# Backward scan: when the context tile's gate rows are loaded, where the output norm scales o, and which half is turned first

## The chip, the cores and the metric

The kernel runs on one core of a Trainium2 chip. It uses the core's engines: TensorE (PE) for matrix products and transposes (its weight loads are shown apart as PEld), VectorE (DVE), ScalarE (ACT) and GpSimd (POOL) for elementwise work, and SyncE (SP), which issues all DMAs. The metric is device microseconds of the whole program, measured over several runs; the profile is one more execution, taken by the hardware profiler.

## The reference

One layer of a hybrid backbone over 17 tiles of 128 tokens: tile 0 is context, tiles 1 to 16 are latent tokens. For each group of tokens:

```python
def block(x, s0, mod, n_chunks, ...):
    sh1, sc1, ga1, sh2, sc2, ga2 = mod
    h = rmsnorm(x, norm_mix_l) * (1.0 + sc1) + sh1
    o, s_new = mixer(h, s0, n_chunks, ...)
    x = x + ga1 * o
    h = rmsnorm(x, norm_ffn_l) * (1.0 + sc2) + sh2
    x = x + ga2 * (jnp.square(jax.nn.relu(h @ w_ff1_l)) @ w_ff2_l)
    return x, s_new
```

and the end of the mixer, which is the part that the change is about:

```python
    o_a, s_new = delta_bidir(q, k, v, g2, beta2, s0)      # DeltaNet, forward and backward
    o_a = rmsnorm(o_a, o_norm_l) * jax.nn.silu(gate.reshape(B, T, H_A, DV))
    ...
    o_b = u * mixed.reshape(B, T, D_B).astype(u.dtype)    # gated MLP over chunks
    out = jnp.concatenate([o_a.reshape(B, T, D_A).astype(h.dtype), o_b.astype(h.dtype)], axis=-1)
    return out @ w_out_l, s_new
```

Context tokens are modulated with another vector than latent tokens, so their gate row `ga1` is another one. `x` is 128 x 1024 a tile; `o_a` and `o_b` are 128 x 512 each, four heads (or groups) of 128.

## The kernel before

The program has three stages. The first projects all tokens and stores what the scans need in DRAM. The second is the scan: a forward pass over the tiles, then a backward pass. The third is the MLP, some 1,300 us of dense products. Products in single precision are made of three matmuls each (L220 to L222: high by high, low by high, high by low), so every operand is split into a rounded high part (on ACT) and the rest (on DVE).

The scan works in units, one for a tile and a direction: unit 0 and unit 1 are the context tile's two directions, units 2 to 17 go forward over the tiles 1 to 16, units 18 to 33 backward over 16 to 1. Each unit has a chain of four steps (`u["scan"]`) that carries the state, and a preparation made for two units together (`pair`): the triangular inverse, by doubling. For each width w of 2, 4, 8, 16 and 32 a level has two steps. The first multiplies on PE (L1173), and DVE copies the result under a mask into P (`copy_predicated`, L1176). The second multiplies with P on PE (L1187, L1193), and ACT copies the results to Y and X. Before the levels there are two turns of X (L1149). The first step for w = 16 is called P16 in what follows, by its copy.

Beside chain and preparation runs "fill": in the forward pass the projections of the gated MLP, in the backward pass the output of each finished tile. For a backward unit of tile t, `o_steps` makes that output:

- `norm` (from L1381) loads ob (the gated MLP's half, from DRAM), squares o on ACT and computes the norm's factors rr, the power by -0.5 on POOL (L178).
- `scaled` (L1396) makes the four factors complete (L1398, a 128 x 4 instruction) and multiplies o by factor and gate, in four instructions, one a head (L1400).
- `trans(0)` turns o, `trans(1)` turns ob: four transposes on PE into a PSUM bank (L1413), the high part on ACT (L1417), the low part on DVE (L1418). `trans(0)` also issues the loads of x (L1409).
- `proj(n, k0)`, eight steps: two halves n of 512 columns, four steps each, over the eight pieces k of the turned halves (0 to 3 are o's, 4 to 7 ob's). The last step of a half multiplies by the gate row into `tmp` (L1437), adds to x (L1438) and stores (L1440).

The gate row of latent tiles is loaded once (`ga1`). For the context tile (`cond(t) == 0`) the last step of each half loads a row of its own with `wrow` (L213): one row of 512 values to all 128 partitions, 256 KB in the tile.

PSUM banks come from `pj()`, which alternates between two pools of two banks, named pm and pj in the profile. Tiles of 512 columns in SBUF come from one pool of 49 (`wp`, tag "w"), which also holds the projection weights.

The order is written as due times. Each step is an event with a time in units: unit i's chain lies near i. A unit's output steps lie at i + 1.0 + part * 0.38, with the parts that `o_steps` returns, and its eight `proj` steps at i + 1.69 to i + 2.69. In that measure P16 of the pair of units i and i + 1 is due at 0.0625 after an odd unit's time, its second step at 0.1875; after an even unit's time the two turns of X lie there. The context tile's output steps are due at 17.9 + part * 0.4 and its `proj` steps from 17 + 1.5 to 17 + 2.68. `emit` issues the events in order of their times. A step without a matmul that is not "fill" is put behind the first matmul of the latest chain or preparation step before it (`hist[-1]`), on whichever engine it runs; a fill step's first matmul is put behind that one too. Within these bounds a planner with a simulated timeline fixes the order of each engine's instructions, earlier-issued ones first among those that are ready; on the chip each engine's queue then runs in that order. SP issues DMAs in its own such order, and a DMA that waits (for a buffer or for an earlier store) holds up those behind it.

Of the kernel before, what the change touches and what calls it, by code (L numbers as in the profile page):

```python
# [14 lines left out]
ALU = mybir.AluOpType  # L15
# [4 lines left out]
D = 1024  # L20
KT = D // P
# [3 lines left out]
H = 4  # L25
# [37 lines left out]
def hybrid_step(  # L63
# [7 lines left out]
    V, A, G, T = nc.vector, nc.scalar, nc.gpsimd, nc.tensor  # L71
# [3 lines left out]
    def xrow(t):  # L75
        return x_prompt[0] if t == 0 else x_sample[0, (t - 1) * P : t * P, :]
# [4 lines left out]
    def cond(t):  # L81
        return 0 if t == 0 else 1

    def f32(ap):
        return ap.bitcast(F32)
# [6 lines left out]
    mod_d = dp.tile([2, 6 * D], F32, name="mod_d")  # L92
# [56 lines left out]
    rq = cp.tile([P, NT, H], F32, name="rq")  # L149
# [24 lines left out]
    def rsqrt_cols(out, ss, n, scale, eps):  # L174
        t = smp.tile([P, 72], F32, tag="rsq", name="rsq", bufs=2)
        np_ = ss.shape[0]
        V.tensor_scalar(out=t[:np_, :n], in0=ss, scalar1=scale, scalar2=eps, op0=ALU.mult, op1=ALU.add)  # L177
        G.tensor_tensor(out=out, in0=t[:np_, :n], in1=nhalf[:np_, :n], op=ALU.pow)  # L178
# [28 lines left out]
    def w512(name, dt=F32):  # L207
        return wp.tile([P, 512], dt, tag="w", name=name)

    def wrow(row):  # L210

        t = w512("row")
        load(out=t, in_=row.to_broadcast([P, 512]))  # L213
        return t

    def mm3(ps, trip, first=True, last=True, more=False):

        n = len(trip)
        for i, (lh, ll, rh, rl) in enumerate(trip):
            T.matmul(ps, lh, rh, start=first and i == 0, stop=False, skip_group_check=more)  # L220
            T.matmul(ps, lh, rl, start=False, stop=False, skip_group_check=more)  # L221
            T.matmul(ps, ll, rh, start=False, stop=last and i == n - 1, skip_group_check=more)  # L222
# [58 lines left out]
    with ExitStack() as ph:  # L281
# [5 lines left out]
        def pj(dt=F32):  # L287
            return ppj.tile([P, 512], dt, tag="pj", name="pj", bufs=3)
# [471 lines left out]
        for bi in range(len(BLOCKS)):  # L760
# [8 lines left out]
            for n, (gi, h) in enumerate(order):  # L769
                u = us[n] if bi == 0 and n < 3 else feature_tile(blk, bi, gi, h)  # L770
# [156 lines left out]
    with ExitStack() as ph:  # L927
# [421 lines left out]
        ga1 = []  # L1349
# [26 lines left out]
        def o_steps(du):  # L1376
            t = du["t"]
            out = []
            u = {}

            def norm():  # L1381
                du["ob"] = w512("ob")
                load(out=du["ob"], in_=ob_d[t * P : (t + 1) * P, :])
                o, ga = du["o"], du["ga"]
                ss = smp.tile([P, 4], F32, tag="oss", name="oss")
                junk = fp.tile([P, P], BF16, tag="junk", name="junk", bufs=1)
                for h in range(H):
                    A.activation(junk, o[:, h, :], AF.Square, accum_out=ss[:, h : h + 1])
                r2 = smp.tile([P, 4], F32, tag="r2", name="r2")
                rr = smp.tile([P, 4], F32, tag="rr", name="rr")  # L1390
                V.tensor_tensor(out=r2, in0=rq[:, t, :], in1=rq[:, t, :], op=ALU.mult)
                V.tensor_tensor(out=r2, in0=r2, in1=ss, op=ALU.mult)
                rsqrt_cols(rr, r2, 4, 1.0 / P, EPS)
                u["rr"] = rr

            def scaled():  # L1396
                o, ga, rr = du["o"], du["ga"], u["rr"]
                V.scalar_tensor_tensor(out=rr, in0=rr, scalar=0.5, in1=rq[:, t, :], op0=ALU.mult, op1=ALU.mult)  # L1398
                for h in range(H):
                    V.scalar_tensor_tensor(out=o[:, h, :], in0=o[:, h, :], scalar=rr[:, h : h + 1],  # L1400
                                           in1=ga[:, h * P : (h + 1) * P], op0=ALU.mult, op1=ALU.mult)

            def trans(half):
                def f():
                    if half == 0:
                        u["H"], u["L"] = [], []
                        u["x"] = [w512("x"), w512("x")]
                        for n in range(2):
                            load(out=u["x"][n], in_=xrow(t)[:, n * 512 : (n + 1) * 512])  # L1409
                    src = du["o"] if half == 0 else du["ob"].rearrange("p (h d) -> p h d", h=H)  # L1410
                    ps = pj().rearrange("p (h d) -> p h d", h=H)
                    for h in reversed(range(H)):
                        T.transpose(ps[:, h, :], src[:, h, :], ident)  # L1413
                    hs = hp.tile([P, 4, P], F32R, tag="h", name="oH")
                    ls = hp.tile([P, 4, P], F32R, tag="h", name="oL")
                    scale = 0.5 if half else vec[:, 68:69]
                    A.activation(hs, ps, AF.Copy, scale=scale)  # L1417
                    V.scalar_tensor_tensor(out=ls, in0=ps, scalar=scale, in1=f32(hs), op0=ALU.mult, op1=ALU.subtract)  # L1418
                    u["H"] += [hs[:, i, :] for i in range(4)]
                    u["L"] += [ls[:, i, :] for i in range(4)]  # L1420
                return f

            def proj(n, k0):
                def f():
                    if k0 == 0:
                        u["ps"] = pj()
                    for k in (k0, k0 + 1):
                        mm3(u["ps"], [(u["H"][k], u["L"][k]) + WO[n][k]], first=k == 0,
                            last=k == KT - 1)
                    if k0 == KT - 2:  # L1430
                        sl = slice(n * 512, (n + 1) * 512)
                        tmp = fp.tile([P, 512], F32, tag="ug" if n else "vg", name="tmp")
                        ga = ga1[n]
                        if cond(t) == 0:
                            ga = wrow(mod_d[0:1, 2 * D + n * 512 : 2 * D + n * 512 + 512])
                        x = u["x"][n]
                        V.tensor_tensor(out=tmp, in0=u["ps"], in1=ga, op=ALU.mult)  # L1437
                        V.tensor_tensor(out=x, in0=x, in1=tmp, op=ALU.add)  # L1438
                        du["x2"] = u["x"]
                        store(out=x2_d[t * P : (t + 1) * P, sl], in_=x)  # L1440
                return f

            for n in range(2):
                for k0 in range(0, KT, 2):
                    out.append(proj(n, k0))
            return [(0.0, norm, "fill"), (0.45, scaled, None), (0.7, trans(0), "fill"), (0.95, trans(1), "fill")], out

        def swap_right():
            right.close()
# [28 lines left out]
        for i, u in enumerate(units):  # L1478
# [9 lines left out]
            if c == 0:  # L1488
# [3 lines left out]
                n = len(steps)  # L1492
# [48 lines left out]
        at(NT + 0.5, lambda: first_state(NT + 1, 1))  # L1541
        at(NT + 0.3, lambda: o_loads(units[1]))
        first, second = o_steps(units[1])
        for part, st, kind in first:
            at(NT + 0.9 + part * 0.4, st, kind)
# [65 lines left out]
    class Unit:  # L1611
# [6 lines left out]
        def load(self, i, kh):  # L1618
            for q in range(2):
                self.raw[i, kh, q] = r = w512("raw")  # L1620
                r0, c0 = kh * 512 + q * 256, self.jp * 512 + i * 256
                load(out=r.rearrange("p (a c) -> p a c", a=2),
                     in_=w_ff1[0, r0 : r0 + 256, c0 : c0 + 256].rearrange("(a p) c -> p a c", p=P))
# [234 lines left out]
    rows = {}  # L1858
# [102 lines left out]
    half = [p for p, e in enumerate(seq) if e[1] == NP][0]  # L1961
# [16 lines left out]
    for p, (o, n, m) in enumerate(seq):  # L1978
        u = units[n]
# [126 lines left out]
```

## Time and profile before

| | |
|---|---|
| median of 3 runs | 2584.34 us (2582.85 to 2585.54) |
| profiled execution | 2586.25 us, span of its instructions 2584.5 us |
| instructions in the profile | 43725 |
| mean granted TensorE clock | 0.997 |
| ACT, POOL busy over the span | 1193.5 us (46%), 296.7 us (11%) |
| backward scan with its outputs | about 885 to 1250 us of the span |

The span runs from the first to the last instruction. An engine is busy while an instruction of its own runs; waiting and issuing DMAs do not count. In a row of the timeline stand start, duration, engine, line, operation, output and inputs, shape and count; in brackets how long the engine had been idle before it, and whose end it seems to have waited for. Rows of SPq are DMA issues: their duration is that of the issue, not of the transfer. In a row of waits stand the waiting engine and line, what it waited for, the total in us, how often, and the longest.

### The profile page before, as it was taken

The page shows a single profiled execution, that of the slowest core. Times are in us where ns is not written, and L with a number is a line of the kernel's source. Part 1 is how long each engine was busy: PE and PEld are TensorE (multiplying, and loading weights), DVE is VectorE, ACT ScalarE, POOL GpSimd, SP SyncE. Part 2 cuts the span into 40 slices and gives each one's busy share as a digit, 9 for nine tenths or more (in the row PEclk, how much of TensorE's full clock was granted, in tenths as well). Part 3 has the DMA queues.
Part 4 walks back from the last instruction along what each step waited for, and adds up shares of the span by engine and source line. Part 5 has one row for each costly group of instructions (what it writes and reads, how often), then busy time and mean ns, then how long its engine had stood idle before and what let it go on. Part 6 is the DMA issues. An engine that isn't in the chain of part 4 may idle for free.

```text
span 2584.5 us, 43725 instructions
## 1 busy us (share of the span) xinstructions
PE 2544.6 (98%) x15296; PEld 2135.4 (83%) x15296; DVE 1785.2 (69%) x3524; ACT 1193.5 (46%) x2758; POOL 296.7 (11%) x512
## 2 busy tenths in 40 slices
PE   8999999999999999999999999999999999999998
PEld 4899999788888778788888888888888888888887
DVE  5776746667667778896588787677785445685874
ACT  3755545554545556763254553333343333243441
POOL 3112112222222222231000000000000000000000
PEclk9999999999999999999999999999999999999999
DMA  8876637755555757996678788545599778786773
GB/s 285 286 233 199 190 128 224 241 162 169 172 168 173 220 185 240 294 309 219 250 227 238 226 277 295 153 136 160 165 299 317 275 257 295 248 258 213 231 251 105
DMA packets 533859, 579.77 MB, mean 224 GB/s; under 512 B 35500, under 2 KB 366684, under 8 KB 530054
## 3 DMA queue, kind: packets, MB, share of 16 engines
q1 hardware_dynamic: 533638, 576.98, 70.0%
q8 instruction: 120, 1.97, 0.3%
q14 instruction: 101, 0.83, 0.1%
HBM read 397.62 MB, written 179.22 MB: 223 GB/s over the span
## 4 chain that ended last, share of the span: by engine, by line
PE 56%; DVE 1%; issue 1%; POOL 0%; DMA 0%; ACT 0%; DVEq 0%; POOLq 0%; ACTq 0%
PE f L220 17%; PE f L221 17%; PE f L222 17%; PE pj L220 1%; PE pj L222 1%; PE pj L221 1%; PE f L856 0%; PE pd L992 0%; PE pd L1096 0%; PE pd L1060 0%; PE pd L1097 0%; DVE o L1400 0%; PE pm L1413 0%; DVE vt L1054 0%; PE f L270 0%
## 5 line engine op out<-in xcount | busy, mean ns | idle before, releaser
L220 PE MATMUL f<-hop,zH 128*128 128x512 f32 x960 | 373.2, 389 | 0.0
L222 PE MATMUL f<-hop,zL 128*128 128x512 f32 x960 | 373.1, 389 | 0.0
L221 PE MATMUL f<-hop,zH 128*128 128x512 f32 x960 | 373.1, 389 | 0.0
L220 PE MATMUL f<-hop,wH 128*128 128x512 f32 x896 | 351.4, 393 | 0.0
L221 PE MATMUL f<-hop,wH 128*128 128x512 f32 x896 | 348.9, 390 | 0.0
L222 PE MATMUL f<-hop,wL 128*128 128x512 f32 x896 | 344.3, 390 | 0.0
L1600 ACT CAST zH<-zraw 128x512 fp32r<-128x512 f32 x240 | 146.7, 620 | 292.3 <-DMA zraw<-s_d 95.9
L1594 DVE TENSOR_TENSOR zL<-zraw,zH 128x512 fp32r<-128x512 f32 x240 | 162.6, 688 | 78.2 <-ACT zH L1600 65.8
L222 PEld LDWEIGHTS f<-hop,zL 128*128 128x128 f32 x960 | 180.2, 188 | 37.4
L221 PEld LDWEIGHTS f<-hop,zH 128*128 128x128 f32 x960 | 180.2, 188 | 37.3
L220 PEld LDWEIGHTS f<-hop,zH 128*128 128x128 f32 x960 | 180.2, 188 | 37.3
L222 PEld LDWEIGHTS f<-hop,wL 128*128 128x128 f32 x896 | 168.2, 188 | 35.7
L220 PEld LDWEIGHTS f<-hop,wH 128*128 128x128 f32 x896 | 168.5, 188 | 34.0 <-issue 0.9
L221 PEld LDWEIGHTS f<-hop,wH 128*128 128x128 f32 x896 | 168.5, 188 | 32.1
L222 PE MATMUL pj<-kH,wL 128*128 128x386 f32 (+2 forms) x568 | 190.5, 335 | 0.0
L220 PE MATMUL pj<-kH,wH 128*128 128x386 f32 (+2 forms) x568 | 189.2, 336 | 0.6 <-DVE kH L487 0.3
L221 PE MATMUL pj<-kL,wH 128*128 128x386 f32 (+2 forms) x568 | 189.3, 333 | 0.0
L178 POOL TENSOR_TENSOR r<-rsq,nhalf 128x1 f32<-128x1 f32 (+1 forms) x38 | 22.9, 603 | 1352.7 <-DVE rsq L177 1352.7
L1747 ACT CAST wH<-s 128x512 fp32r<-128x512 f32 x96 | 58.8, 620 | 173.8 <-DVE s L1594 160.6
L537 DVE SCALAR_TENSOR_TENSOR cv<-pj,vec,cv 128x384 f32<-128x384 f32 (+2 forms) x164 | 87.3, 540 | 56.1 <-ACT cv L534 54.8
L220 PEld LDWEIGHTS pj<-kH,wH 128*128 128x128 f32 x568 | 107.1, 189 | 5.2 <-issue 4.7
L221 PEld LDWEIGHTS pj<-kL,wH 128*128 128x128 f32 x568 | 107.4, 189 | 0.6
(408 smaller groups left out, 5720.1 us busy)
## 6 DMA issues: line engine op xcount, KB each, us to landing
zraw<-z_d SPq DMA_DIRECT2D x212, 256.0 KB
raw<-in_w_ff_dram SPq DMA_DIRECT2D x128, 256.0 KB
hop<-hop_d SPq DMA_DIRECT2D x28, 1024.0 KB
z_d<-c SPq DMA_DIRECT2D x96, 256.0 KB
zraw<-s_d SPq DMA_DIRECT2D x96, 256.0 KB
raw<-in_w_mod_dram SPq DMA_DIRECT2D x80, 256.0 KB
r<-in_w_ff_dram SPq DMA_DIRECT2D x80, 256.0 KB
s_d<-s SPq DMA_DIRECT2D x64, 256.0 KB
```

The source lines that it names most:

```text
L178: G.tensor_tensor(out=out, in0=t[:np_, :n], in1=nhalf[:np_, :n], op=ALU.pow)
L220: T.matmul(ps, lh, rh, start=first and i == 0, stop=False, skip_group_check=more)
L221: T.matmul(ps, lh, rl, start=False, stop=False, skip_group_check=more)
L222: T.matmul(ps, ll, rh, start=False, stop=last and i == n - 1, skip_group_check=more)
L537: V.scalar_tensor_tensor(out=cv[:, o : o + m], in0=ps[:, s + sh : s + sh + m], scalar=convw[:, w, j : j + 1], in1=cv[:, o : o + m], op0=AL ...
L1594: V.tensor_tensor(out=out, in0=a, in1=b, op=op)
L1600: A.copy(h, src)
L1747: A.copy(h, s2)
```

## The change

It has three parts. The context tile's two gate rows are loaded in `trans`, together with the first transposes and ahead of x's loads, and `proj` uses them from there. The completion of the norm's factors becomes a step of its own (`factors`, part 0.42), and the scaling of o moves from part 0.45 to 0.52; in time after an odd unit that is from 0.171 to 0.198, past the second step of level 16 at 0.1875. And ob is turned first (`trans(1)`, part 0.7), o second (`trans(0)`, part 0.9 in place of 0.95 for the second turn); x's loads go with whichever is first. The lists of turned pieces are filled by place, so that the projection still reads o's pieces as 0 to 3.

```diff
+            def factors():
+                rr = u["rr"]
+                V.scalar_tensor_tensor(out=rr, in0=rr, scalar=0.5, in1=rq[:, t, :], op0=ALU.mult, op1=ALU.mult)
+
             def scaled():
                 o, ga, rr = du["o"], du["ga"], u["rr"]
-                V.scalar_tensor_tensor(out=rr, in0=rr, scalar=0.5, in1=rq[:, t, :], op0=ALU.mult, op1=ALU.mult)
                 for h in range(H):
                     V.scalar_tensor_tensor(out=o[:, h, :], in0=o[:, h, :], scalar=rr[:, h : h + 1],
                                            in1=ga[:, h * P : (h + 1) * P], op0=ALU.mult, op1=ALU.mult)
 
             def trans(half):
                 def f():
-                    if half == 0:
-                        u["H"], u["L"] = [], []
+                    if half:
+                        u["H"], u["L"] = [None] * KT, [None] * KT
+                        if cond(t) == 0:
+                            u["rows"] = [wrow(mod_d[0:1, 2 * D + n * 512 : 2 * D + n * 512 + 512]) for n in range(2)]
                         u["x"] = [w512("x"), w512("x")]
                         for n in range(2):
                             load(out=u["x"][n], in_=xrow(t)[:, n * 512 : (n + 1) * 512])
...
-                    u["H"] += [hs[:, i, :] for i in range(4)]
-                    u["L"] += [ls[:, i, :] for i in range(4)]
+                    for i in range(4):
+                        u["H"][half * 4 + i], u["L"][half * 4 + i] = hs[:, i, :], ls[:, i, :]
                 return f
...
-                        ga = ga1[n]
-                        if cond(t) == 0:
-                            ga = wrow(mod_d[0:1, 2 * D + n * 512 : 2 * D + n * 512 + 512])
+                        ga = u["rows"][n] if cond(t) == 0 else ga1[n]
...
-            return [(0.0, norm, "fill"), (0.45, scaled, None), (0.7, trans(0), "fill"), (0.95, trans(1), "fill")], out
+            return [(0.0, norm, "fill"), (0.42, factors, None), (0.52, scaled, None), (0.7, trans(1), "fill"),
+                    (0.9, trans(0), "fill")], out
```

## Prediction

> **What bounds the kernel now.** I read the page first, for the engine that fills the span, then the windows by stage, then TensorE's waits in the stage that the change touches, then the timeline of each wait.
>
> ```profile
> PE 2544.6 (98%) x15296; PEld 2135.4 (83%) x15296; DVE 1785.2 (69%) x3524; ACT 1193.5 (46%) x2758; POOL 296.7 (11%) x512
> ```
>
> TensorE (PE) is busy for 98% of the span. A change that removes no matmul can win only where PE stands still or runs on a lower clock. The windows (columns: stretch, length, PE, PEld, DVE, ACT, POOL busy, granted clock, DMA share, GB/s) say where: the first row is the backward scan, the second the sum over four stretches from 1260 to 2560 us, the MLP.
>
> ```profile
> 860.00:1260.00 400.00, 385.56 (x3207) 319.52 (x3206) 311.92 (x682) 232.16 (x600) 94.13 (x100) 0.99 0.74 236
> sum 1300.00, PE 1300.00 PEld 1079.96 DVE 891.65 ACT 511.62 POOL 15.20; mean PE 325.00 PEld 269.99 DVE 222.91 ACT 127.90 POOL 3.80
> ```
>
> The MLP has no PE gap at all, so what the scan saves reaches the end undiminished. The scan's second half idles PE for 400 − 385.56 = 14.4 us. Its two longest entries of waits (total, times, longest):
>
> ```profile
> PE pd L1187 <- DVE P L1176: 6.1, 7, 1.4
> PE pm L1413 <- DVE tmp L1437: 5.5, 1, 5.5
> ```
>
> These are the change's targets: 11.6 of the 14.4 us.
>
> **The change part by part.**
>
> *The context tile's gate rows.* The one wait of 5.5 us, in the timelines of PE, DVE and SyncE (SP):
>
> ```profile
> 914.08 0.39 PE L222 MATMUL pm<-wH,oL 128*128 128x512 f32 x1
> ```
> ```profile
> 919.83 0.41 PE L1173 MATMUL pd<-Y,AH 128*128 128x64 f16 x8
> 925.74 0.47 PE L1413 MATMUL pm<-ident,ob 128*128 128x128 f32 x1 [5.50 <-DVE tmp L1437]
> ```
> ```profile
> 924.99 0.69 DVE L1437 TENSOR_TENSOR tmp<-pm,row 128x512 f32<-128x512 f32 x1 [5.79 <-DMA row<-mod_d]
> ```
> ```profile
> 913.86 0.45 SPq L1330 DMA_DIRECT2D ob_d<-ug  x1
> 917.11 0.33 SPq L1383 DMA_DIRECT2D ob<-ob_d  x1
> 917.49 1.66 SPq L1371 DMA_DIRECT2D of<-of_d  x1
> 919.20 0.42 SPq L1374 DMA_DIRECT2D ga<-gate_d  x1
> 919.67 0.43 SPq L213 DMA_DIRECT2D row<-mod_d  x1
> ```
>
> The first half of the context's output projection is complete in its pm bank at 914.5. The product that empties the bank (tmp, L1437) needs the gate row, and that load is issued only at 919.67, in SP's queue behind the ob load, which stands until the ob store has landed (913.86 to 917.11, 3.25 us). The row takes 924.99 − 919.67 = 5.3 us. Meanwhile the next tile's ob transpose has no bank, and PE idles 5.50 us behind it.
>
> The change issues both rows at the context's first transposes, where SP stood like this:
>
> ```profile
> 888.46 0.81 SPq L1409 DMA_DIRECT2D x<-in_x_prompt_dram  x2
> 889.36 0.38 SPq L213 DMA_DIRECT2D row<-mod_d  x1
> 889.89 0.33 SPq L184 DMA_DIRECT2D raw<-in_w_out_dram  x1
> 890.50 0.33 SPq L957 DMA_DIRECT2D gr<-g_d  x1
> 892.63 0.33 SPq L1009 DMA_DIRECT2D vt<-vt_d  x1
> ```
>
> Two more issues cost 2 × 0.43 = 0.86 us of SP. Raw and gr go that much later; from vt on the gap of 1.8 us between 890.83 and 892.63 swallows it, and without that gap the queue behind would be 0.86 us late. Issued near 889, at 5.3 us, the rows are there by 895, some 19 us before 914.5. The row wait goes whole.
>
> What is late next? The ob transpose itself: its load left at 917.11. With the store's 3.25 us it lands at 920.4, with the row's 5.3 at 922.4. PE comes to this turn between its place today (end of L1173, 920.24) and the place of the first turn, about 918.0. So what remains lies between 0.2 and 4.4 us; I take 0.5, nearest to the store (same tensor, same queue, just before) and to the later place, since PE's order has the projection's second half to run before. Of 5.5 us, **5.0** go.
>
> *The clock behind that wait.* PE's clock fell with it (same columns as above):
>
> ```profile
> 922.00:924.00 2.00, 0.00 (x0) 0.00 (x0) 0.00 (x0) 0.00 (x0) 0.00 (x0) 0.69 0.79 182
> 924.00:926.00 2.00, 0.26 (x1) 0.27 (x2) 1.01 (x2) 0.00 (x0) 0.00 (x0) 0.50 0.96 357
> 926.00:928.00 2.00, 2.00 (x21) 1.93 (x21) 2.00 (x4) 1.11 (x4) 0.00 (x0) 0.50 0.21 79
> 928.00:930.00 2.00, 2.00 (x9) 1.62 (x8) 1.94 (x4) 2.00 (x6) 0.00 (x0) 0.60 0.35 131
> ```
>
> From 925.74 to 928 the clock is 0.5, then 0.60 on average to 930. Work lost: 2.26 × 0.5 + 2.0 × 0.40 = **1.9 us**. Whether all of it returns depends on what idle time is left there; with 0.5 us in place of 5.5 I count all of it. The Trainium skill ("TensorE: Matmul & The Clock Gate", Part 1) says that the clock is halved after a whole idle window of 3.4 us, and that these windows run freely. The trace agrees as to size: 5.5 us idle did it. By that rule an idle time of 5.5 us holds a whole window only in some executions; then the other timed runs of before never paid the 1.9.
>
> *Scaling behind P16's copy.* In every second tile the masked copy of level 16 (P, L1176) stands behind the four scalings of o:
>
> ```profile
> 1005.41 0.68 DVE L875 TENSOR_TENSOR opL<-ev,opH 128x512 fp32r<-128x512 f32 x1
> 1006.01 1.14 DVE L1400 SCALAR_TENSOR_TENSOR o<-o,rr,ga 128x128 f32<-128x128 f32 x4
> 1007.06 0.69 DVE L1176 CAST_PREDICATED P<-om,pd 128x512 f16<-128x512 uint16 x1
> 1007.66 0.69 DVE L875 TENSOR_TENSOR opL<-ev,opH 128x512 fp32r<-128x512 f32 x1
> ```
> ```profile
> 1004.58 0.41 PE L1173 MATMUL pd<-Y,AH 128*128 128x64 f16 x8
> ```
> ```profile
> 1006.05 0.40 PE L222 MATMUL pm<-wH,oL 128*128 128x512 f32 x1
> 1007.80 0.36 PE L1187 MATMUL pd<-P,X 128*128 128x64 f16 x7 [1.35 <-DVE P L1176]
> ```
>
> P's input (L1173) is done on PE at 1004.99, and DVE has no gap before P. Take the scalings out and P starts 1007.06 − 1006.01 = 1.05 us earlier; L1187's wait falls from 1.35 to 0.30. TensorE's waits on P from 1000 to 1100, and from 905 to 1190 us:
>
> ```profile
> PE pd L1187 <- DVE P L1176: 4.1, 3, 1.4
> ```
> ```profile
> PE pd L1187 <- DVE P L1176: 5.0, 6, 1.4
> ```
>
> Beside the three waits of 1.35 there are 5.0 − 4.1 = 0.9 us in three short ones. At most 3 × 1.05 + 0.9 = 4.1 us go. But the order on DVE is planned: with the scalings barred, the planner may put the second opL (1007.66, 0.60 us to the next) ahead of P in the three tiles; then 3 × 0.45 + 0.9 = 2.3. I take the middle, **3.2**. The scalings end where P ended, near 1007.7; the transposes of o were at 1010.6, and P plus scalings take as long in either order, so nothing behind on DVE moves. The factors become a step of their own, without one more instruction, and stay ahead of P.
>
> *ob turned first.* In the other half of the tiles, the odd ones (scalings on DVE; on PE the second turn of X and the turns of o and ob):
>
> ```profile
> 1031.84 1.67 DVE L1400 SCALAR_TENSOR_TENSOR o<-o,rr,ga 128x128 f32<-128x128 f32 x3
> ```
> ```profile
> 1029.46 0.40 PE L1149 MATMUL pd<-ident,X 128*128 128x128 f16 x4
> ```
> ```profile
> 1033.76 0.60 PE L1413 MATMUL pj<-ident,o 128*128 128x128 f32 x4
> 1034.19 0.60 PE L1413 MATMUL pj<-ident,ob 128*128 128x128 f32 x4
> ```
>
> The scalings end at 1033.5, and o's turn gets 0.43 us more room. Nothing is added: the same eight transposes, two ACT copies and two DVE differences. But the projection reads o's pieces first, and they now come second. That is covered by other PE work except in the last tile:
>
> ```profile
> 1239.26 0.50 PE L222 MATMUL pj<-wH,oL 128*128 128x512 f32 x1 [0.34 <-DVE oL L1418]
> ```
> ```profile
> 1238.46 0.75 DVE L1418 SCALAR_TENSOR_TENSOR oL<-pm,vec,oH 128x512 fp32r<-128x512 f32 x1
> 1239.12 0.68 DVE L1437 TENSOR_TENSOR tmp<-pj,row 128x512 f32<-128x512 f32 x1
> 1239.71 0.68 DVE L1418 SCALAR_TENSOR_TENSOR oL<-pm,oH 128x512 fp32r<-128x512 f32 x1
> ```
>
> There o's oL moves from the first to the second place of DVE, by 0.6 (tmp falls behind) to 1.25 us (it does not), and PE with it. Cost between 0.6 and 1.2; I take **0.7**.
>
> *Sum.* 5.0 + 1.9 + 3.2 − 0.7 = 9.4 us. The profiled execution took 2586.25 us (span 2584.5) and would take 2576.9. The median of the three runs is 1.9 lower, 2584.34; from there 9.4 off gives **2574.9 us**. With all terms at their good ends (5.3 + 1.9 + 4.1 − 0.6 = 10.7) it is 2573.6; a changed order may also take some of the 2.8 us of idle time that I left alone, so 2571 at the bottom; with P at 2.3 and the tail at 1.2, 2576.3, and a wait of 2 us at ob, 2578.
>
> **The rivals.**
>
> *The clock term is not in the timed runs.* For: they spread over 2.7 us, and one execution's trace shows its fall only after some 2 us of idle time. Against: nothing but that spread. The gain is then 7.5, the time 2576.8. This is what the skill's free-running window would give.
>
> *ob's load takes the row's place.* For: ob is now wanted first, and this load alone waits for a store of the stage just ended. If it takes the row's 5.3 us and PE wants it at 918.0, it waits 4.4 us, and the clock may fall all the same: 1.1 + 3.2 − 0.7 = 3.6 us gained, 2580.7, within 0.2%. Against: DMA is less busy without the row in it. The Trainium skill ("DMA: Bandwidth & Descriptors", Anatomy of one DMA) puts a transfer at 2.0 us and its bytes at 436 GB/s, on GpSimd's path; that would be an estimated 2.6 us for these 256 KB, and the sum would be 0.5 us better. The row's 5.3 us speaks against leaning on it.
>
> *It doesn't do what it says.* The rows take buffers that the last gate-MLP matmuls release one by one; if a buffer comes free only after 908 or the planner issues the rows late, the wait stays. Then the P part can be all: 2584.34 − 2.5 = 2581.8. Against: the row at 889.36 found a buffer at that place today.
>
> *Slower: o's scalings miss their turn in the odd tiles.* They are now queued after a later step, on a DVE without gaps, and PE, in order, stands at o's turn. The point is 1034.19 − 1033.5 = 0.7 us of room. Beyond it each us costs one in each of 8 tiles; to be slower by 5.2 us it must cost 14.6 in all, 1.8 a tile, so the scalings must end 2.5 us later than today: 2589.5. Against: their new predecessor there, the second turn of X, is at 1029.46, ahead of them already.
>
> **How the numbers follow.** Forecast 0.60 (2571 to 2578), clock term absent 0.13 (2576.8), late ob 0.11 (2580.7), rows not early 0.08 (2581.8), slower 0.08 (2589.5). The bound of 0.2%, about what a measurement of this kernel can tell from no change, is 5.2 us: 2579.2. Faster 0.60 + 0.13 = 0.73, same 0.11 + 0.08 = 0.19, slower 0.08. For 8 in 10 the range takes in the forecast, the absent clock term and the late ob: 2570.5 to 2581.
>
> **What would show it.** Row: two gate-row loads issued near 890, no wait of L1413 on tmp, clock 1.00 in all windows of the scan. P: L1187's waits of 1.35 gone or below 0.9, L1400 after L1176. Turn: L1413's ob ahead of o; the last tile's oL wait near 1 us. I am wrong if a new wait of over 2 us stands at L1413, if the scan's idle time stays above 9 us, or if PE gaps show up in the MLP.

## The result and the profile after

The changed kernel takes 2577.70 us (median of 7 runs, 2576.03 to 2580.97) against 2584.34 us before (7 runs on the same chip): 6.6 us less, a ratio of 0.9975 with a 95% interval of 0.9965 to 0.9985. The forecast was 2574.9, so the direction and the range held, and 2.8 us of the expected 9.4 are missing. The profiled execution took 2576.43 us (span 2574.7), at a mean granted clock of 0.999 where before had 0.997. One execution among the runs below (e4_rows_turn, 3600.34 us at a mean granted clock of 0.654) is left out of every median and interval.

Two executions also differ by chance before the scan's second half, where the code is the same. So traces are compared over a **stretch** that holds all the changed work: from the first product of vt with T in unit 17 (L1060) to the MLP's first product (output f). Its two ends on PE, before:

```profile
868.51 1.14 PE L1060 MATMUL pd<-vt,T 128*128 128x128 f32 x8
...
1249.82 0.39 PE L220 MATMUL f<-hop,wH 128*128 128x512 f32 x1
```

and after:

```profile
864.18 1.14 PE L1060 MATMUL pd<-vt,T 128*128 128x128 f32 x8
...
1239.97 0.39 PE L220 MATMUL f<-hop,wH 128*128 128x512 f32 x1
```

381.31 us became 375.79: 5.5 us less by the trace, within the interval of the timed runs. The window of the scan's second half, after:

```profile
860.00:1260.00 400.00, 389.75 (x3208) 323.06 (x3208) 312.30 (x686) 235.09 (x608) 110.20 (x99) 1.00 0.76 244
```

PE's idle time there fell from 14.4 to 10.25 us, and the clock stands at 1.00. With the 1.9 us that the slow clock had cost, that is 6.1 us, close to the 5.5. TensorE's five longest entries of waits in this window, after (total, times, longest):

```profile
PE pj L1418 <- DVE o L1403: 3.8, 3, 1.3
PE pd L1187 <- DVE P L1176: 3.3, 9, 1.1
PE pm L1418 <- DMA ob<-ob_d: 1.0, 1, 1.0
PE pd L1149 <- DVE X L1141: 0.8, 1, 0.8
PE pj L221 <- DVE wL L192: 0.7, 1, 0.7
```

The two targets are smaller: the wait of 5.5 us on tmp is gone, and P fell from 6.1 to 3.3 us. The longest entry is new: PE stands at the turn of o (L1418, which was L1413), 3.8 us in three waits, behind the scaling of o (L1403, was L1400). That is the gain that is missing, and the experiments ask where it comes from.

The gate rows did what was said. The DMA issues of SP, after:

```profile
884.00 0.80 SPq L213 DMA_DIRECT2D row<-mod_d  x2
...
913.10 0.32 SPq L1383 DMA_DIRECT2D ob<-ob_d  x1
```

Both rows leave at 884.00, long before the first is used. What is late next is the load of ob, issued at 913.10 for a turn that starts 3.11 us later, on PE:

```profile
916.21 0.66 PE L1418 MATMUL pm<-ident,ob 128*128 128x128 f32 x4 [0.99 <-DMA ob<-ob_d]
```

P16 in an even tile, on PE and then on DVE, after:

```profile
996.17 0.40 PE L222 MATMUL pm<-wH,oL 128*128 128x512 f32 x1
996.87 0.39 PE L1187 MATMUL pd<-P,X 128*128 128x64 f16 x8 [0.30 <-DVE P L1176]
```
```profile
995.53 0.68 DVE L875 TENSOR_TENSOR opL<-ev,opH 128x512 fp32r<-128x512 f32 x1
996.13 0.68 DVE L1176 CAST_PREDICATED P<-om,pd 128x512 f16<-128x512 uint16 x1
996.73 0.68 DVE L875 TENSOR_TENSOR opL<-ev,opH 128x512 fp32r<-128x512 f32 x1
```

P now follows the first opL directly; the second opL stayed behind it, and the scalings come later. The wait is 0.30 us, the number forecast.

The odd tile is where it went wrong. Unit 23's output, on ACT, DVE and PE, after:

```profile
1008.96 0.62 ACT L874 CAST opH<-y 128x512 fp32r<-128x512 f32 x1 [0.70 <-DMA hop_d<-opH]
1009.61 1.51 ACT L859 ACTIVATE ev<-pj,b,a 128x128 f32<-128x128 f32 x4
...
1011.83 0.31 ACT L1388 ACTIVATE junk<-o 128x128 bf16<-128x128 f32 x1
...
1012.58 1.12 ACT L1136 CAST AH<-KK 128x512 f16<-128x512 f32 x2
1013.61 0.31 ACT L1388 ACTIVATE junk<-o 128x128 bf16<-128x128 f32 x1
...
1013.91 1.48 ACT L859 ACTIVATE ev<-pm,b,a 128x128 f32<-128x128 f32 x4
1015.28 0.31 ACT L1388 ACTIVATE junk<-o 128x128 bf16<-128x128 f32 x1
```
```profile
1016.45 0.15 DVE L1392 TENSOR_TENSOR r<-r,oss 128x4 f32<-128x4 f32 x1
...
1020.50 0.16 DVE L1398 SCALAR_TENSOR_TENSOR rr<-rr,rq 128x4 f32<-128x4 f32 x1 [0.24 <-POOL rr L178]
1021.02 2.02 DVE L849 TENSOR_SCALAR x<-x,r 128x512 f32<-128x512 f32 x2 [0.36 <-POOL r L178]
...
1023.56 1.13 DVE L1403 SCALAR_TENSOR_TENSOR o<-o,rr,ga 128x128 f32<-128x128 f32 x4
```
```profile
1024.74 0.66 PE L1418 MATMUL pj<-ident,o 128*128 128x128 f32 x4 [1.24 <-DVE o L1403]
```

The four squares of o (L1388; the second, from 1012.27, is left out), which feed the norm, no longer stand together as they did in unit 23 of before, on ACT:

```profile
1022.24 0.31 ACT L1388 ACTIVATE junk<-o 128x128 bf16<-128x128 f32 x1 [0.35 <-DVE o L1108]
...
1023.54 0.31 ACT L1388 ACTIVATE junk<-o 128x128 bf16<-128x128 f32 x1
...
1023.85 1.12 ACT L1136 CAST AH<-KK 128x512 f16<-128x512 f32 x2
```

In after, ACT first waits 0.70 us in a copy opH (L874, an operand of the MLP made from an earlier tile), and two other pieces of work, AH and ev, are put among the squares. (In units 25 and 27 the squares are split in the same way; there the copy ahead of them waits 0.56 and 0.58 us, which the trace puts down to tmp on DVE and not to a store.) The last square starts at 1015.28, the first product with the squares (L1392) at 1016.45, POOL's power is waited for at 1020.50, and the scalings end at 1024.69. PE has been at o's turn since 1023.50. DVE does not stand for the last square: it goes from X (1015.78, 0.75 us) to the product without a gap, so the late squares act through the order that was planned for DVE. The power on POOL took 2.06 us there (from 1018.41), against 1.02 us in before, e4_rows_turn and e9_op_behind; DVE stood 0.24 and 0.36 us for POOL, and no run shows why it took longer.

### The profile page after: what moved, and what is told of

The parts are those of the page before. It is cut to its first block, busy times and chain, and to the rows that moved or that the text cites. A ratio compares the mean times of both kernels' runs of the same rounds, so it can differ in the third digit from the quotient of the medians.

```text
span 2574.7 us, 43713 instructions
## 1 busy us (share of the span) xinstructions
PE 2542.1 (99%) x15296; PEld 2134.4 (83%) x15296; DVE 1781.9 (69%) x3524; ACT 1192.5 (46%) x2758; POOL 313.9 (12%) x512
## 4 chain that ended last, share of the span: by engine, by line
PE 55%; DVE 1%; issue 1%; DMA 0%; ACT 0%; POOL 0%; SPq 0%; DVEq 0%; POOLq 0%; ACTq 0%
PE f L220 17%; PE f L221 17%; PE f L222 17%; PE pj L220 1%; PE pj L222 1%; PE pj L221 1%; PE f L856 0%; PE pd L992 0%; PE pd L1096 0%; PE pd L1097 0%; DMA gr<-g_d 0%; PE pm L1418 0%; DMA x<-in_x_sample_dram 0%; PE pd L1060 0%; PE f L270 0%
## 5 line engine op out<-in xcount | busy, mean ns | idle before, releaser
L220 PE MATMUL f<-hop,zH 128*128 128x512 f32 x960 | 373.2, 389 | 0.0
L222 PE MATMUL f<-hop,zL 128*128 128x512 f32 x960 | 373.1, 389 | 0.0
L221 PE MATMUL f<-hop,zH 128*128 128x512 f32 x960 | 373.1, 389 | 0.0
L221 PE MATMUL f<-hop,wH 128*128 128x512 f32 x896 | 348.9, 390 | 0.0
L221 PEld LDWEIGHTS f<-hop,zH 128*128 128x128 f32 x960 | 180.2, 188 | 37.3
L221 PEld LDWEIGHTS f<-hop,wH 128*128 128x128 f32 x896 | 168.6, 188 | 32.2
L221 PE MATMUL pj<-kL,wH 128*128 128x386 f32 (+2 forms) x568 | 189.3, 333 | 0.0
L221 PEld LDWEIGHTS pj<-kL,wH 128*128 128x128 f32 x568 | 107.4, 189 | 0.6
```

## The experiments

The times of the runs, each against runs of the kernel before on the same chip, and the stretch of each trace between the same two instructions (381.31 before, 375.79 after):

| run | what it is | median us (before's) | ratio, 95% interval | stretch us |
|---|---|---|---|---|
| e1_rows | rows early only | 2579.06 (2583.03) | 0.9983 [0.9974, 0.9992] | 375.88 |
| e2_scale | scaling moved only | 2576.23 (2583.03) | 0.9972 [0.9962, 0.9983] | 377.39 |
| e3_rows_scale | both, o turned first | 2575.74 (2583.03) | 0.9967 [0.9954, 0.9979] | 373.19 |
| e4_rows_turn | rows and ob first, scaling at its old place | 2577.31 (2583.03) | 0.9978 [0.9968, 0.9987] | 375.66 |
| e5_late_o | after, odd tiles' o turned later | 2578.55 (2583.66) | 0.9983 [0.9975, 0.9992] | 379.65 |
| e6_squares | after, odd tiles' squares together | 2577.46 (2583.66) | 0.9976 [0.9967, 0.9984] | 376.60 |
| e7_rows_scale | e3 again | 2573.85 (2583.66) | 0.9962 [0.9949, 0.9974] | 373.21 |
| e8_after | after again | 2577.42 (2583.66) | 0.9975 [0.9966, 0.9984] | 376.13 |
| e9_op_behind | e6, copies opH behind the squares too | 2575.07 (2584.24) | 0.9963 [0.9951, 0.9976] | 371.31 |
| e10_rows_scale | e3 once more | 2574.29 (2584.24) | 0.9962 [0.9948, 0.9975] | 373.79 |

The change itself repeats: e8_after's stretch is 0.3 us from the first one's, and the three stretches of the kernel of e3 lie within 0.6 us. The medians of two kernels that are within 2 us cannot be told apart by these intervals; stretches that differ by more than that 0.6 us, and their waits, can.

**e1_rows: the first part alone.** The kernel before with

```diff
                     if half == 0:
                         u["H"], u["L"] = [], []
+                        if cond(t) == 0:
+                            u["rows"] = [wrow(mod_d[0:1, 2 * D + n * 512 : 2 * D + n * 512 + 512]) for n in range(2)]
...
-                        ga = ga1[n]
-                        if cond(t) == 0:
-                            ga = wrow(mod_d[0:1, 2 * D + n * 512 : 2 * D + n * 512 + 512])
+                        ga = u["rows"][n] if cond(t) == 0 else ga1[n]
```

> Only the context tile's gate rows move: they are loaded with its first transposes; scaling and order of the turns stay as before. Measure by the trace: the stretch from the first T-by-vt product of unit 17 (L1060) to the first MLP matmul, 381.3 us before and 375.8 after. Theory A (the whole net gain is the row wait and the clock behind it): stretch 374 to 376 us, row wait gone, clock 1.00 in the scan, the three waits of 1.35 us on P still there; time as after's or 1 us below, some 2577. Rival B (each part brings its share, as forecast): the row part alone brings the 6.9 us forecast for it, and this kernel is 2 to 3 us slower than the full change would be with its forecast 3.2; by the trace it would then lie near 374.4, which is also what A allows, so what tells them apart is the sign against after: under A not slower than after, under B slower.

At unit 20's chain the lead over before had grown by 6.84 us: the 5.0 and the 1.9 of the forecast, nearly to the tenth. That it is so exact is luck in part: 5.33 of the 5.50 us went, and the next wait on P grew from 0.38 to 0.98. A unit later 1.07 of it was gone, and the stretch is 5.43 us shorter. The waits, e1_rows, same window:

```profile
PE pd L1187 <- DVE P L1176: 7.2, 10, 1.4
PE pm L1415 <- DVE o L1400: 0.9, 1, 0.9
```

The three waits of 1.35 us on P are still there, and one tile's o is late. So the rows gain 6.8 us at their place, and PE, which comes earlier, meets work of other engines that does not.

**e2_scale: the second part alone.** The kernel before with `factors` split off as in the change, o still first:

```diff
-            return [(0.0, norm, "fill"), (0.45, scaled, None), (0.7, trans(0), "fill"), (0.95, trans(1), "fill")], out
+            return [(0.0, norm, "fill"), (0.42, factors, None), (0.52, scaled, None), (0.7, trans(0), "fill"),
+                    (0.95, trans(1), "fill")], out
```

> Only the factors' own step and the later scaling of o; o is still turned first, the rows are loaded late as before. Theory A (the scaling's gain on P is given back at o's turn): the three waits on P fall from 1.35 to 0.3 us (3.1 us), and waits of 1 to 2 us appear at o's turn in the odd tiles, more of them or longer ones than after's three of 1.25, since o is now also turned at the earlier place; stretch 380 to 383 us, the row wait still 5.5. Rival B (it is the order of the turns that makes o late, not the scaling): no waits at o's turn, stretch 378 us, some 3 us faster than before.

The waits of 1.35 are 0.30, and none stands at the odd tiles' turn of o. The two longest waits, e2_scale:

```profile
PE pd L1187 <- DVE P L1176: 2.8, 5, 1.1
PE pm L1416 <- DVE tmp L1440: 2.2, 1, 2.2
```

The second is the row wait, with 2.25 of 5.50 us left. tmp starts where it did, 56.3 us into the stretch (56.5 in before), but PE gets to the turn of ob at 54.8 in place of 51.7: the changed order puts other work ahead of it. So the scaling's move gives nothing back in the odd tiles by itself, and a part of the row gain comes with it. The profiled execution lost 3.4 us to a fall of the clock (last section), so its stretch without that is an estimated 374.0.

**e3_rows_scale, e7 and e10: the first two parts without the third.** The two edits above together.

> The change without its third part: rows early, scaling behind P16's copy, o still turned first. Theory A: as the row part alone on the row, and waits at o's turn as in the kernel with the scaling alone; stretch 375 to 378 us, the same as after or slower by 1 to 2 us. Rival B (ob first is what costs): 372 to 373 us, about 3 us faster than after.

> Rows early and scaling behind P16's copy, o turned first: the fastest by its trace so far (stretch 373.2 against 375.8), once more, beside the full change. If the order of the turns costs what the traces say, 2.6 us, its median is 1.5 to 3.5 us below that of the full change on the same chip; if that is an accident of one profiled execution, they are equal within 1 us.

Three traces agree: 373.19, 373.21 and 373.79 us, 7.5 to 8.1 less than before and 2.0 to 2.6 less than after. On one chip the median of e7 is 3.6 us below that of e8_after (2573.85 against 2577.42), at the upper end of what was expected. The waits, e7_rows_scale:

```profile
PE pd L1187 <- DVE P L1176: 2.4, 6, 1.1
...
PE pj L222 <- DVE oL L1423: 0.4, 1, 0.4
```

Between these rows stand four that concern R, wL and X; none is at o's turn. (In e3 and e10 one of under 0.5 us stands there, in unit 19.) Leaving the third part out beats the whole change.

**e4_rows_turn: the first and third part.** The kernel after with the factors back in `scaled`:

```diff
-            return [(0.0, norm, "fill"), (0.42, factors, None), (0.52, scaled, None), (0.7, trans(1), "fill"),
-                    (0.9, trans(0), "fill")], out
+            return [(0.0, norm, "fill"), (0.45, scaled, None), (0.7, trans(1), "fill"), (0.9, trans(0), "fill")], out
```

> The change without its second part: rows early, ob turned first, scaling of o at its old due time. Theory A (the moved scaling makes o late): no waits at o's turn, the three waits of 1.35 us on P back, stretch 375 to 376.5 us, equal to after within 1 us. Rival B (ob first makes o late, through the order that the planner then picks): waits at o's turn and on P both there, stretch 378 to 379 us, some 3 us slower than after.

The three waits of 1.35 on P are back, as they must be, and units 23, 25 and 27 have no wait at o's turn; one of 0.7 us stands in unit 19. So ob first alone does not make o late in those tiles, and neither does the scaling's move alone. It takes both. Unit 23 shows how, on DVE and PE, e4_rows_turn (its stretch starts at 864.44):

```profile
1022.72 1.67 DVE L1400 SCALAR_TENSOR_TENSOR o<-o,rr,ga 128x128 f32<-128x128 f32 x3
```
```profile
1025.05 0.60 PE L1415 MATMUL pj<-ident,o 128*128 128x128 f32 x4
```

The scalings end at 1024.39, 0.66 us before PE comes. Counted from the start of the stretch, PE comes to this turn 1.29 us earlier in after than here, 1.05 us of which is what it no longer waits for P in the tile before, and the scalings end 0.56 us later. So the 0.66 us of room becomes a wait of 1.2 us. With the rows early, the stretch is 375.9 with neither of the other two parts (e1), 373.2 to 373.8 with the scaling moved, 375.7 with ob first and 375.8 to 376.1 with both: ob first gives nothing by itself and takes away what the scaling gave.

**e5_late_o: give o more time.** After, with o's turn later in the odd tiles:

```diff
-                    (0.9, trans(0), "fill")], out
+                    (1.3 if t % 2 else 0.9, trans(0), "fill")], out
```

> The full change, with o turned later in the odd tiles (part 1.3 in place of 0.9). In the full change o's turn waits three times 1.25 us for the scaling that ends as it starts. Theory C (only the place of the turn in TensorE's order is wrong, the scaling's end is harmless): the three waits vanish, P's waits stay at 0.3, stretch from the first L1060 product of unit 17 to the first MLP matmul 372 to 373 us against 375.8 (after) and 373.2 (rows and scaling without the turn). Rival D (the late scaling drags everything: VectorE's chain is what is late): the wait moves to the next user, oL or the projection, or P of the next level; stretch 374.5 to 376.

The wait at o's turn is gone, and PE waits longer at the next thing, P, behind the same late scalings on DVE. Waits and one window, e5_late_o:

```profile
PE pd L1187 <- DVE P L1176: 9.7, 11, 1.9
```
```profile
1032.00:1034.00 2.00, 2.00 (x21) 2.00 (x17) 2.00 (x4) 1.82 (x4) 0.00 (x0) 0.52 0.79 230
```

Three waits of 1.87 to 1.89 us took the place of three of 1.25, and behind two of them the clock was halved. This was the slowest of the eleven executions (2586.97 us). The clock cost an estimated 3.4 us of its 379.65 (0.52 and 0.63 over two windows of 2 us, 0.56 and 0.59 behind the other wait); without that it is some 376.2, as long as after's. Moving PE's turn is no remedy: what is late is DVE.

**e6_squares: make the scaling earlier.** After, with the odd tiles' `norm` issued earlier (part -0.5), and the copies to AH and the evictions to ev held behind its last square on ACT by an order-only dependency:

```diff
+        def after_squares(fn):
+            start = len(tc.nc.cur_bb.bb.instructions)
+            fn()
+            for x in tc.nc.cur_bb.bb.instructions[start:]:
+                if "n" in sq and x.engine == mybir.EngineType.Activation:
+                    tc.add_manual_dep(x, sq["n"], mybir.DependencyInfo(
+                        mybir.DependencyClass.NoSync, mybir.DependencyReason.DATA), reason="order")
...
+                after_squares(lambda: [A.copy(mine("AH", c), u["KK"]) for c, u in enumerate(us)])
...
+                    st[3:5] = [lambda f=f: after_squares(f) for f in st[3:5]]
```

> The full change, with the four squares of o in the odd tiles kept together on ScalarE: the copies to AH and the evictions of h2's transposes are put behind them. In the full change these come between the squares of units 23, 25 and 27 and not with o turned first. Theory E (the split squares make the norm's factors late, the factors the scaling, the scaling o's turn): scaling some 2.5 us earlier, three waits at o's turn gone, stretch 372 to 374 us; AH is up to 0.9 us later, which may cost some tenths at R or T. Rival F (the squares are no cause; the scaling is late because VectorE has other work planned ahead of it): the waits stay within 0.5 us of 1.25.

Within the stretch the scalings of unit 23 start 2.1 us earlier than in after and end 1.3 us earlier, and o's turn no longer waits. But the copy opH still stands first on ACT and waits for its store, and now AH is late behind the squares, and with it X. Waits, e6_squares (its lines from there on are 9 to 11 higher; L1158 is the turn of X, L1149 in the others):

```profile
PE pd L1158 <- DVE X L1150: 4.7, 4, 1.5
PE pd L1196 <- DVE P L1185: 3.9, 11, 1.1
```

3.9 of the 4.7 us are in units 23, 25 and 27. The wait moved to a third place. The sum did not fall: 376.60.

**e8_after** is the change once more.

> The full change again, beside the others on one chip: ratio to before 0.9965 to 0.9985 as measured; its trace has the three waits of 1.25 us at o's turn again, stretch 375.8, since one program has one order. If the stretch differs by over 0.5 us, the differences between the other kernels' stretches of this size mean nothing.

Its three waits at o's turn are 1.24 us each, and its stretch is 0.34 us longer than the first one's. Its other short waits are not all the same: the 0.7 us on wL is absent, and two waits on R (0.61 and 0.21 us) have come in its place.

**e9_op_behind: take the delay out at its head.** e6 with the copies opH held behind the squares too, so that ACT need not stand in them first:

```diff
-                    st[3:5] = [lambda f=f: after_squares(f) for f in st[3:5]]
+                    st[3:] = [lambda f=f: after_squares(f) for f in st[3:]]
```

> The kernel after, with the odd tiles' four squares of o kept together on ScalarE as in e6_squares and, beyond that, the copies opH of the MLP's operand steps (L874) held behind the squares too, so that ScalarE no longer stands 0.7 to 0.95 us ahead of the squares for a store of hop_d. Nothing is left out of the computation. Theory (the late squares, held up by that waiting copy, make the odd tiles' scaling late, and o's turn only has to bear it because ob is first): the waits of TensorE at o's turn (3.8 us in three) go and do not come back at X's turn or at P; the stretch from unit 17's first vt product to the MLP's first product, 375.8 to 376.1 after, falls by 3 to 3.8 us to 372.0 to 373.1, that of e3 and e7 (373.2); median near 2574.5, ratio near 0.996. Rival (ob's transposes ahead of o's take the room, whatever ScalarE does): a wait of over 1 us stays in each of units 23, 25 and 27, at o's turn, X's turn or P, as in e5_late_o and e6_squares, and the stretch stays at 375.5 to 376.6, ratio 0.9975.

> The kernel of e3 and e7 once more (rows early and the scaling moved, o turned first), beside e9_op_behind on the same chip, to compare the two. Stretch 373.2 as in both, ratio 0.996 to 0.997. If the order of the turns alone is not what costs, e9_op_behind comes to within 1 us of this one; if it is, e9_op_behind stays 2 to 3 us longer.

The three longest waits, e9_op_behind:

```profile
PE pd L1196 <- DVE P L1185: 3.6, 9, 1.1
PE pd L1158 <- DVE X L1150: 0.8, 1, 0.8
PE pm L1429 <- DMA ob<-ob_d: 0.7, 1, 0.7
```

Nothing waits at o's turn, and X's turn is back at its single 0.8 us. The same places as in the odd tile of after, on ACT, DVE and PE:

```profile
1015.25 0.31 ACT L1397 ACTIVATE junk<-o 128x128 bf16<-128x128 f32 x1
...
1015.56 0.61 ACT L874 CAST opH<-y 128x512 fp32r<-128x512 f32 x1
1016.07 1.13 ACT L1145 CAST AH<-KK 128x512 f16<-128x512 f32 x2
```
```profile
1015.96 0.15 DVE L1403 TENSOR_TENSOR r<-r,oss 128x4 f32<-128x4 f32 x1
...
1023.72 1.67 DVE L1414 SCALAR_TENSOR_TENSOR o<-o,rr,ga 128x128 f32<-128x128 f32 x3
```
```profile
1026.04 0.60 PE L1429 MATMUL pj<-ident,o 128*128 128x128 f32 x4
```

This trace runs 3.5 us later than after's from its start (867.72 against 864.18 at unit 17), so the product with the squares (here DVE's L1403) at 1015.96 is 4.0 us earlier within the stretch than after's 1016.45. The scalings end at 1025.39, PE comes at 1026.04, and nothing waits. The stretch is 371.31 us: 4.5 less than after's and 10.0 less than before's, even more than the 372.0 to 373.1 that the theory gave. It is also 1.9 to 2.5 below the kernel without the third part, whose waits on R (2.2 us in e7) it does not have. The timed runs cannot tell these two apart (2575.07 and 2574.29 on one chip).

## Why the prediction was right, and where it failed

**The rows: right, 5.0 forecast.** The loads leave at 884, the wait of 5.50 is gone, and 0.99 us stay at ob's load where 0.5 was taken. The load was waited for 3.11 us after its issue, close to the 3.25 of the store that had served as nearest row. A wait of 0.65 us on a weight split (L221, wL) follows it that I had not named; e8_after, the same program, does not have it.

**The clock: right, 1.9 forecast.** All windows of the stretch are at 1.00, and e1_rows gained 6.84 us where 5.0 + 1.9 was said. The rival by which the timed runs never paid it is not borne out: of the 23 runs of before beside e1 to e4, 19 had a mean clock of 0.997 or 0.998 and four one of 0.999, which six of the seven runs of after had. The mean is that of the whole program, so it does not count this one fall by itself. The prediction read from the trace that an idle time of 5.5 us brought the fall; less was enough (last section).

**Scaling behind P16: the mechanism right, the size 3.2 nearly.** The three long waits went from 1.35 to 0.30, the good end of what was open, as the second opL stayed behind P. The 0.9 us of short waits did not go: the trace of after shows 1.7 us on P from 898 to 1182 us where before had 5.0 at the same place. That is 3.3 us gained. Over the whole window it is 2.8 (from 6.1 to 3.3): a wait of 1.1 us at 901 stays, at 897, and one of 0.46 us at 891 is new. All six traces with ob first have the latter, and none with o first.

**ob turned first: this step failed.** It said that o's turn gets 0.43 us more room, and the step before it that nothing behind on DVE moves. Both took the end of the scalings as fixed against PE's turn, at 1033.5 in the odd tile of before. It was not: PE came earlier by what it gained at P, and the new issue order changed ACT's order, so that squares of o that had stood together were spread. The scalings did not come as much earlier as PE, and were too late for it by 1.24 us in unit 23 and 1.25 in 25 and 27. The rival on the other side of the forecast named this very wait, with a price in eight tiles, and I dismissed it because its new predecessor on PE, X's second turn, was ahead already. That looked only at the last bar in the chain, and not at what feeds the scalings: squares, power, factors. Only three tiles paid, 3.7 us in all, not eight.

That the cause is the late chain and not the order of the turns is shown by e9_op_behind: with ob still first, the squares kept together and the waiting copies behind them, all three waits go. e6 shows that the squares alone bring the scalings early enough for o's turn, but then AH is late. e5 and e6 show the delay at two other places, P and X's turn: as long as ACT and DVE were late, PE waited in both. That it takes the scaling's move and the new order of turns together is shown by e2, e3 and e4. Why the planner puts the copies first when both are there was not settled; no run isolates it.

**The last tile: forecast as 0.7 lost, but nothing is.** oL's wait of 0.34 us in before is absent from the waits of after, while e7, with o first, has it (0.4). The forecast kept the two turns back to back, as they were in before (1236.72 and 1237.15). In after they are 3.0 us apart (1224.05 and 1227.03) with products of the projection between them, so the two oL no longer stand in each other's way.

**The sum.** The forecast's 5.0 + 1.9 + 3.2 - 0.7 = 9.4 against the trace: rows 5.50 - 0.99 - 0.65 = 3.9, clock 1.9, P over the whole window 2.8, tail 0.3, o's turn -3.7: 5.2. Two short waits of before that are shorter or gone, on Y (0.49 to 0.38 us) and R (0.28 us), add 0.4, and the stretch shows 5.5. The time fell within the forecast's own range (2571 to 2578) with one term missing that is larger than the P term. That is luck in part: the upper end was reckoned from a P term of 2.3, a tail of 1.2 and a wait of 2 us at ob, and none of these came. The sign named for being wrong had appeared: idle time in the scan stayed above 9 us, at 10.25.

## What to carry to other kernels

When a step is moved in a planned order, do not take the end of the work that feeds it as fixed: follow its inputs back over every engine, and ask what the planner may now slip in between. If a wait moves from one place to the next when each is given priority, as in e5 and e6, look for the late link upstream of all of them, here copies on ACT that were put ahead of urgent squares and among them. A wait that is removed brings PE earlier to its next turn, so look how much room that turn has. Try the parts of a change singly and in pairs: two parts that do no harm alone can together lose what one of them gains.

## What the hardware showed

The clock can fall behind less idle time than the 5.50 us of before. In before itself it fell near 922.8 (1.24 us at half make the 0.69 of the window from 922 to 924), 2.5 us after PE had stopped at 920.24 and 3 us before it went on; it was back near 929.6, 6.8 us later. In the profiled execution of e2_scale PE stood for 2.25 us and no more. That wait on PE, and the windows (the granted clock is third from the right):

```profile
922.68 0.65 PE L1416 MATMUL pm<-ident,ob 128*128 128x128 f32 x4 [2.25 <-DVE tmp L1440]
```
```profile
922.00:924.00 2.00, 1.32 (x13) 0.93 (x13) 2.00 (x4) 0.60 (x2) 0.00 (x0) 1.00 1.04 393
924.00:926.00 2.00, 1.60 (x4) 0.83 (x3) 2.00 (x4) 0.57 (x1) 0.23 (x1) 0.50 0.76 292
...
930.00:932.00 2.00, 2.00 (x12) 1.86 (x11) 0.84 (x3) 0.00 (x0) 0.00 (x0) 0.79 0.81 260
```

The clock halves at 924, 1.3 us after PE is back at work, and stays so to about 930.8 (0.84 us at half make the 0.79 of the last window): 6.8 us, which cost 3.4 us of work. Of the eight executions of this kernel, six with a mean clock of 0.999 took 2575.7 to 2576.3 us, and two with 0.998 took 2579.2 and 2579.4: 3.3 us more, about what the fall in the trace cost (the profiled execution is one of the two). So it seems that the fall comes in some executions and not in others. In e5_late_o two of three equal waits brought one (1.87 us each; near 1032.1 and 1124.2, for 3.4 us each) and the third, of 1.89 us, did not: the length of a wait alone does not decide it. The Trainium skill ("TensorE: Matmul & The Clock Gate", Part 1) has the clock fall after a whole idle window of 3.4 us, with windows that run freely. That equal waits differ, and that the falls here lasted 3.4 us or twice that, agrees with free windows; that 2.25 us idle did it, and 1.87 us in e5_late_o, does not agree with a whole idle window, and here the measurement decides. The waits of 1.25 us in after did not bring it in the profiled execution.
